# Down products in another order, constants inside the product stream, and idle products during the load, in a hybrid encoder block

## The chip, the core and the metric

The kernel runs on one core of one Trainium2 chip. Its time is the device time of one launch, in microseconds (us); smaller is better. Five engines work beside each other, each on its own queue of instructions in program order: PE (TensorE, matrix products and transposes), DVE (VectorE), ACT (ScalarE), POOL (GpSimd) and SP, whose queue here issues most of the DMA transfers between HBM and the on-chip memory. An instruction waits, by semaphore, for what it needs, and everything behind it on its engine waits with it.

## The reference

One block of a bidirectional encoder over 1024 tokens of 1024 features, all in float32:

```
x = x + 1/2 * SwiGLU_1(RMSNorm(x))          # FFN 1: gate, up: 1024 -> 2816; down: 2816 -> 1024
p = RMSNorm(x) @ W_in                       # latents, mLSTM inputs, gates, two branch gates
A = MLA(p)                                  # latent attention, 8 heads, rotary key from positions
B = mLSTM(p)                                # forward and backward chunked scans, 4 heads
x = x + (sigmoid(g_A) * (A @ Wa) + sigmoid(g_B) * (B @ Wb)) @ W_out
x = x + 1/2 * SwiGLU_2(RMSNorm(x))          # FFN 2, as FFN 1
x = RMSNorm(x)
SwiGLU(h) = (silu(h @ w_gate) * (h @ w_up)) @ w_down
```

The rotary tables are sines and cosines of positions times 16 frequencies.

## The kernel before

**Precision.** A float32 matrix product is made of three products of halves: each operand is split into a high part H (an ACT copy to the type fp32r) and a low part L (the difference, on DVE), and PE adds H·H, H·L and L·H into one PSUM bank. So every operand costs an ACT and a DVE instruction before PE can use it: for weights these are L250 and L251, for the activations L367 and L368, for the down products L594 and L595.

**Products.** The large products use Strassen and Winograd's scheme: a product of 2 by 2 blocks is made of seven products, numbered 1 to 7, and sums of blocks. Tokens 0 to 511 (tiles of 128 tokens, t = 0 to 3) are the first row of blocks, t = 4 to 7 the second.

**Stages**, in order of the trace: load, norm and transposes of x (0 to 24 us); FFN 1 gate and up (24 to 460); FFN 1 down (460 to 679); narrow projections, latents, gates (to about 840); mLSTM (to 1100); attention (to 1346); branch products and merge (to 1440); the output projection, called the merged down product (1443 to 1518); FFN 2 gate and up (1532 to 1960), FFN 2 down and the last norm (to 2182).

**Load.** `rms_x` norms a token tile: a square on ACT, a small chain over DVE and POOL, and one multiplication by scale and weight, L112 on DVE, or for t = 1, 3, 5 in two later stages L109 and L110 on POOL. `combine_x` transposes the tile on PE (L363, eight 128x128 transposes against an identity), splits it (L367, L368), and for t < 4 keeps a plain copy s = H + L (POOL, L375); for t ≥ 4 it forms Winograd's sums T1 to T4 from the transposed tile and that copy. `begin(j)` issues the first products of column block j (L260 to L262, X and weight split by L250 and L251), which need only tiles t < 4. So the four late tiles are turned between calls of `begin`, and what follows them needs T2 of the last tile.

**Gate and up.** `gate_up` runs a list of items, each a group of products on one PSUM bank, and prepares the splits of weights four items ahead. A hook may be called ahead of an item.

**Constants.** `constants()` makes the rotary tables and the like: 14 small DVE instructions behind a transfer of the positions (from L684), some ACT functions, all in a tile called raw of which there are two. It is called before `pairs()`, the main part of gate and up.

**Down.** `down` makes seven products of 4 banks (one per 128 tokens, 512 columns). For FFN each product has 11 steps of 12 matmuls; for the merged product 4 steps. In each step SP loads a pair of operands, ACT and DVE split it (L594, L595), and L602 issues 12 matmuls. The order is 1, 6, 2, 5, 7, 3, 4. When a bank is done, DVE adds it to x (L624). Product 3 completes t = 0 to 3 and product 4 completes t = 4 to 7; `done(t)` then writes x out and norms the tile, and its transposes follow (L128 for FFN 1, L363 for the merged product). The steps of product 4 carry some transposes of t < 4 in FFN 1. The order of PE's instructions is chosen by a scheduler unless instructions are pinned by `keep_in_program_order`.

PSUM banks come from two groups of four (b0, b1), splits from 6 buffers, the loads from 4 (rw) and 2 (raw).

## Time and profile before

| | us |
|---|---|
| median of 3 runs | 2179.76 (2177.51 to 2180.40) |
| profiled execution | 2183.92 |
| its span, first to last instruction | 2182.1 |
| PE busy in the span | 2107.3 |
| DVE busy | 1520.4 |
| ACT busy | 954.6 |
| POOL busy | 376.5 |
| mean granted clock of PE | 0.988 |

The profile comes from one execution; the 1.8 us that it took beside its span lie before the first and after the last instruction. The clock is a share of full speed, 1 being 2.4 GHz; PE has two levels, 1.2 and 2.4 GHz, so a stretch at 0.75 was half at either. PE is not busy in 2182.1 - 2107.3 = 74.8 us of the span; 11.6 us of that lie behind its last instruction.

### The profile page before, as it was taken

The numbers are of one execution on the slowest core, as the hardware profiler recorded it, in microseconds if no ns is written. First come the engines' busy times: TensorE is split into PE (matmuls) and PEld (weight loads), VectorE is DVE, ScalarE is ACT, GpSimd is POOL, SyncE is SP. The second block draws the span as 40 slices with busy tenths as digits, with TensorE's granted clock in tenths as the row PEclk, the third lists the DMA queues.
The fourth block names the chain that finished last, engine by engine and source line by source line (L and its number), as shares of the span: only waits on it lengthen the run. The fifth ranks groups of instructions, "written<-read, shape, count | busy, mean of one in ns | idle before, by whom it ended". The sixth has DMA issues, their size and how long they took to land.

```text
span 2182.1 us, 27814 instructions
## 1 busy us (share of the span) xinstructions
PE 2107.3 (97%) x10091; PEld 1761.1 (81%) x10091; DVE 1520.4 (70%) x2205; ACT 954.6 (44%) x1493; POOL 376.5 (17%) x319
## 2 busy tenths in 40 slices
PE   6899999999998999999999999998999999999997
PEld 5788888888886888888888888877788888888886
DVE  6788777765476566366658887667788877774565
ACT  5433333334444334544368885235533333324344
POOL 3000000000013655243445442002300000000001
PEclk9999999999998999999999999999999999999999
DMA  8567544486553333222441103975567744557545
GB/s 231 171 209 237 190 164 164 172 305 193 174 193 111 121 111 123 81 88 88 153 150 49 40 11 124 332 258 171 169 216 240 241 157 153 178 206 239 194 147 188
DMA packets 249337, 367.85 MB, mean 169 GB/s; under 512 B 24048, under 2 KB 133488, under 8 KB 249200
## 3 DMA queue, kind: packets, MB, share of 16 engines
q1 hardware_dynamic: 244016, 355.60, 49.5%
q10 hardware_dynamic: 4608, 8.39, 1.0%
q8 instruction: 79, 1.29, 0.2%
q0 software_dynamic: 576, 2.10, 0.2%
q14 instruction: 58, 0.48, 0.1%
HBM read 254.28 MB, written 111.74 MB: 168 GB/s over the span
## 4 chain that ended last, share of the span: by engine, by line
PE 42%; DVE 8%; ACT 3%; issue 2%; DMA 2%; POOL 2%; DVEq 0%; SPq 0%; ACTq 0%; POOLq 0%
PE pb L602 11%; PE pb L261 5%; PE pb L262 5%; PE pb L260 5%; PE pP L1237 2%; PE pav L1245 1%; PE pSc L83 1%; PE pav L1246 1%; DVE s L271 1%; PE pSc L84 1%; PE pSc L85 1%; PE pb L83 1%; PE pb L84 1%; PE pb L85 1%; DVE w L251 1%
## 5 line engine op out<-in xcount | busy, mean ns | idle before, releaser
L602 PE MATMUL pb<-w 128*128 128x512 f32 x2184 | 501.4, 391 | 7.9 <-DVE w L595 7.9
L602 PEld LDWEIGHTS pb<-w 128*128 128x128 f32 x2184 | 410.8, 189 | 95.7 <-DVE w L595 10.3
L595 DVE TENSOR_TENSOR w<-rw,w 128x1024 fp32r<-128x1024 f32 x182 | 222.1, 1227 | 182.3 <-ACT w L594 180.8
L594 ACT ACTIVATE w<-rw 128x1024 fp32r<-128x1024 f32 x182 | 192.7, 1062 | 281.2 <-PE pb L602 262.1
L93 POOL TENSOR_TENSOR rs<-ms,mhalf 128x1 f32<-128x1 f32 (+3 forms) x52 | 61.8, 1193 | 1019.5 <-DVE ms L98 1012.8
L250 ACT ACTIVATE w<-s 128x512 fp32r<-128x512 f32 x176 | 110.8, 629 | 243.5 <-DVE s L267 192.3
L251 DVE TENSOR_TENSOR w<-s,w 128x512 fp32r<-128x512 f32 x176 | 121.6, 691 | 61.3 <-ACT w L250 61.0
L83 PE MATMUL pin<-HH,dH 128*128 128x512 f32 x384 | 152.3, 397 | 0.2 <-DVE TL L1213 0.2
L84 PE MATMUL pin<-HL,dH 128*128 128x512 f32 x384 | 150.9, 393 | 0.0
L85 PE MATMUL pin<-HH,dL 128*128 128x512 f32 x384 | 150.5, 393 | 0.0
L260 PE MATMUL pb<-XH,w 128*128 128x512 f32 x352 | 138.9, 397 | 2.3 <-ACT XH L367 1.3
L260 PE MATMUL pb<-YH,w 128*128 128x512 f32 x352 | 137.9, 394 | 0.7 <-ACT s L412 0.7
L261 PE MATMUL pb<-XL,w 128*128 128x512 f32 x352 | 137.9, 392 | 0.0
L261 PE MATMUL pb<-YL,w 128*128 128x512 f32 x352 | 137.6, 391 | 0.0
L262 PE MATMUL pb<-XH,w 128*128 128x512 f32 x352 | 137.0, 391 | 0.0
L262 PE MATMUL pb<-YH,w 128*128 128x512 f32 x352 | 137.0, 391 | 0.0
L251 DVE TENSOR_TENSOR w<-rw,w 128x512 fp32r<-128x512 f32 x144 | 102.6, 715 | 41.3 <-ACT w L250 41.2
L271 DVE TENSOR_TENSOR s<-pb,s 128x512 f32<-128x512 f32 x152 | 103.5, 686 | 19.4 <-PE pb L262 16.9
L250 ACT ACTIVATE w<-rw 128x512 fp32r<-128x512 f32 x144 | 89.0, 622 | 36.4 <-PE pb L85 12.7
L416 ACT ACTIVATE h<-s 128x512 f32<-128x512 f32 x66 | 41.8, 633 | 120.1 <-DVE s L271 120.1
L1229 POOL TENSOR_SCALAR pe<-pe,ri 128x1024 f32<-128x1024 f32 x64 | 72.0, 1126 | 112.1 <-DVE ri L1228 106.5
L1239 DVE TENSOR_TENSOR PL<-pP,PH 128x512 fp32r<-128x512 f32 x128 | 82.9, 679 | 7.2 <-ACT PH L1238 7.2
(326 smaller groups left out, 4624.9 us busy)
## 6 DMA issues: line engine op xcount, KB each, us to landing
rw<-in_ffn_w_gate SPq DMA_DIRECT2D x54, 512.0 KB, 5.9
rw<-in_ffn_w_up SPq DMA_DIRECT2D x54, 512.0 KB, 5.1
rw<-in_ffn_w_down SPq DMA_DIRECT2D x44, 512.0 KB, 3.8
rw<-f1h SPq DMA_DIRECT2D x77, 256.0 KB, 2.8
rw<-f2h SPq DMA_DIRECT2D x77, 256.0 KB, 2.7
rw<-in_ffn_w_down SPq DMA_DIRECT2D x66, 256.0 KB, 3.0
f1h<-h SPq DMA_DIRECT2D x55, 256.0 KB, 2.4
f2h<-h SPq DMA_DIRECT2D x55, 256.0 KB, 2.3
```

Of the source, the lines that this page charges most:

```text
L83: nc.tensor.matmul(ps, wH, mH, start=start, stop=False)
L84: nc.tensor.matmul(ps, wH, mL, start=False, stop=False)
L85: nc.tensor.matmul(ps, wL, mH, start=False, stop=stop)
L250: nc.scalar.activation(out=H_, in_=src, func=AF.Copy)
L251: return (H_, L_), lambda: nc.vector.tensor_tensor(out=L_, in0=src, in1=f32(H_), op=ALU.subtract)
L260: nc.tensor.matmul(ps, w[0][:, k, :], B[0][:, k, :], start=start and k == 0, stop=False, skip_group_check=True)
L261: nc.tensor.matmul(ps, w[0][:, k, :], B[1][:, k, :], start=False, stop=False, skip_group_check=True)
L262: nc.tensor.matmul(ps, w[1][:, k, :], B[0][:, k, :], start=False, stop=stop and k == 3, skip_group_check=True)
L271: eng.tensor_tensor(out=out, in0=a, in1=b, op=op)
L594: nc.scalar.activation(out=H_, in_=r, func=AF.Copy)
L595: nc.vector.tensor_tensor(out=L_, in0=r, in1=f32(H_), op=ALU.subtract)
L602: nc.tensor.matmul(banks[t], l[:, 0, ts_], r[:, 1, :], start=start and j == 0 and i == 0, stop=stop and j == n - 1 and i == 2, skip_group_ ...
```

## The change

The order of the products in `down` becomes 1, 2, 6, 5, 3, 7, 4: product 3, which completes t = 0 to 3, is fifth instead of sixth, with products 7 and 4 behind it. Product 2 accumulates on the banks of product 1, and product 3 on those of product 5, which are first copied by ACT (as before, but now directly ahead of them). The matmuls of L602 are pinned in program order, the last two steps of products 3 and 4 go bank by bank (`tails=2`). The transposes of t < 4 move into steps of product 7 (FFN 1) or of 7 and 4 (merged product). The multiplications of t = 1, 3, 5 go from POOL to DVE; the copies s in `combine_x` go from POOL to ACT. `constants()` is hooked ahead of the items of j = 6 and has a tile of its own. In FFN 2, `begin(0)` comes ahead of the late tiles, so no `begin` stands behind the last of them. During the load, 29 products of the identity with itself are issued between the transposes (14, 3, 3, 3, 6). Three blocks of narrow columns (`small_cols`) instead of two are issued ahead of the gates.

```diff
 in rms_x callers:   rms_x(t, w, xn_tile(t), t in (1, 3, 5))  ->  rms_x(t, w, xn_tile(t))
...
@@ combine_x
-            p_ = R.bank(1).rearrange("p (k t) -> p k t", k=4)
+            p_ = R.bank(group).rearrange("p (k t) -> p k t", k=4)
...
-            for n, s in zip(("B11", "B21"), kept[i]):
-                nc.gpsimd.tensor_tensor(out=s, in0=f32(X[n][0][:, :, c]), in1=f32(X[n][1][:, :, c]), op=ALU.add)
+            for v, s in zip(ps, kept[i]):
+                nc.scalar.activation(out=s, in_=v, func=AF.Copy)
@@ gate_up
-                    hooks[j]()
+                    in_order(hooks[j])
@@ down, products
-                    nc.tensor.matmul(banks[t], l[:, 0, ts_], r[:, 1, :], start=start and j == 0 and i == 0,
-                                     stop=stop and j == n - 1 and i == 2, skip_group_check=True)
+                    tc.keep_in_program_order(nc.tensor.matmul(
+                        banks[t], l[:, 0, ts_], r[:, 1, :], start=start and j == 0 and i == 0,
+                        stop=stop and j == n - 1 and i == 2, skip_group_check=True))
@@ down
-        u2 = [R.sum() for _ in range(4)]
-        for t in range(4):
-            nc.scalar.activation(out=u2[t], in_=a[t], func=AF.Copy)
+        u2 = copies(a)
+        run(2, a, False, True, each=lambda t: add(xo[t][:, lo], a[t], xo[t][:, lo]))
         b = [R.bank(1) for _ in range(4)]
-        run(6, b, True, True, each=lambda t: into(nc.vector, u2[t], b[t], u2[t], ALU.add))
-        run(2, a, False, True, each=lambda t: add(xo[t][:, lo], a[t], xo[t][:, lo]))
-        c = [R.bank(1) for _ in range(4)]
+
+        def c12_first(t):
+            into(nc.vector, u2[t], b[t], u2[t], ALU.add)
+            add(xo[t][:, hi], u2[t], xo[t][:, hi])
+        run(6, b, True, True, each=c12_first)
+        c = [R.bank(0) for _ in range(4)]
         run(5, c, True, True)
...
+        p5 = copies(c)
+
+        def c12(t):
+            add(xo[t][:, hi], c[t], xo[t][:, hi])
+            done(t)
+        run(3, c, False, True, each=c12, tails=2)
+        d = [R.bank(1) for _ in range(4)]
+        step7, step4 = between()
...
-        run(7, d, True, True, each=c22)
-
-        def c12(t):
-            add(xo[t][:, hi], c[t], xo[t][:, hi])
-            done(t)
-        run(3, c, False, True, each=c12, tails=last, raw=R.raw)
+        run(7, d, True, True, each=c22, step=step7, raw=R.raw)
...
-        run(4, e, True, True, each=c21, step=step, tails=last, raw=R.raw)
+        run(4, e, True, True, each=c21, step=step4, tails=2, raw=R.raw)
@@ FFN 1
-        begin, pairs = gate_up(R, X, *fw1, comb)
+        begin, pairs = gate_up(R, X, *fw1, comb, {6: constants})
...
+        def busy(n):
+            b = R.bank(0)
+            for _ in range(n):
+                tc.keep_in_program_order(nc.tensor.matmul(b[:, 0:P], ident, ident, start=True, stop=True))
+        busy(14)
...
-                    combine_x(R, t, xn.pop(t), X, kept)
+                    combine_x(R, t, xn.pop(t), X, kept, t % 2)
+                    busy(3 if t < 3 else 6)
...
-        constants()
         pairs()
...
-                if t in (5, 6):
+                if t > 4:
                     early[t - 5] = small_cols(t - 5, R.bank(1))
...
-                if 1 <= j < 5:
-                    mix_turn(j - 1)
-            return step
+                if 4 <= j < 8:
+                    mix_turn(j - 4, 0)
+            return step, None
@@ merged product and FFN 2
-            for t in range(4):
-                combine_x(R, t, xn.pop(t), X2, kept)
+            def step7(j):
+                if j == 2:
+                    turn(0, 0)
+
+            def step4(j):
+                if j < 2:
+                    turn(2 * j + 1, 1)
+                if j == 0:
+                    turn(2, 1)
+            return step7, step4
...
+        begin(0)
         for t in range(4, NT):
-            begin(t - 4)
+            begin(t - 3)
             combine_x(R, t, xn.pop(t), X2, kept)
-        begin(4)
         pairs()
```

The rows that follow are of the instruction order of each kernel: line, operation, output <- inputs with buffer numbers, size. Lines from 124 on stand a few numbers higher in the changed kernel.

On DVE, in the load: L112 is the norm's multiplication (into raw, t = 2 and t = 3), L368 makes the low part of a turned tile, L251 that of a weight. Before:

```order
L112 SCALAR_TENSOR_TENSOR raw_316<-x_314,rs_321,nw_258 128x1024
L251 TENSOR_TENSOR w_375<-rw_370,w_375 128x512
L368 TENSOR_TENSOR XL0_240<-pb_301,XH0_239 128x4x128
L251 TENSOR_TENSOR w_394<-rw_372,w_394 128x512
L251 TENSOR_TENSOR w_412<-rw_370,w_412 128x512
L112 SCALAR_TENSOR_TENSOR raw_344<-x_342,rs_349,nw_258 128x1024
L251 TENSOR_TENSOR w_427<-rw_372,w_427 128x512
```

And in the changed kernel:

```order
L112 SCALAR_TENSOR_TENSOR raw_339<-x_337,rs_344,nw_273 128x1024
L98 TENSOR_SCALAR ms_374<-ss_372 128x1
L368 TENSOR_TENSOR XL0_240<-pb_315,XH0_239 128x4x128
L368 TENSOR_TENSOR XL0_240<-pb_320,XH0_239 128x4x128
L112 SCALAR_TENSOR_TENSOR raw_371<-x_369,rs_376,nw_273 128x1024
L251 TENSOR_TENSOR w_409<-rw_404,w_409 128x512
L251 TENSOR_TENSOR w_428<-rw_406,w_428 128x512
```

The multiplication of t = 3 has moved ahead of the first three splits of weights.

On PE, at the end of FFN 1's last product: L602 is the down product into the four banks of t = 4 to 7 (numbers pb_5311 to pb_5314 before), L128 turns the normed tile of t = 4. Before:

```order
L602 MATMUL pb_5311<-w_5564 128x512
L602 MATMUL pb_5312<-w_5564 128x512
L602 MATMUL pb_5313<-w_5564 128x512
L602 MATMUL pb_5314<-w_5564 128x512
L602 MATMUL pb_5311<-w_5565,w_5564 128x512
L602 MATMUL pb_5311<-w_5564,w_5565 128x512
L602 MATMUL pb_5312<-w_5565,w_5564 128x512
L602 MATMUL pb_5312<-w_5564,w_5565 128x512
L602 MATMUL pb_5313<-w_5565,w_5564 128x512
L602 MATMUL pb_5313<-w_5564,w_5565 128x512
L602 MATMUL pb_5314<-w_5565,w_5564 128x512
L602 MATMUL pb_5314<-w_5564,w_5565 128x512
```

And in the changed kernel (banks pb_5423 to pb_5426, of which the one of t = 5, pb_5424, is last):

```order
L128 MATMUL psT_5628<-ident_72,xn_5620 128x128 x4
L128 MATMUL psT_5635<-ident_72,xn_5620 128x128 x4
L602 MATMUL pb_5424<-w_5601 128x512
L602 MATMUL pb_5424<-w_5602,w_5601 128x512
L602 MATMUL pb_5424<-w_5601,w_5602 128x512
L602 MATMUL pb_5424<-w_5608 128x512
L602 MATMUL pb_5424<-w_5609,w_5608 128x512
L602 MATMUL pb_5424<-w_5608,w_5609 128x512
L128 MATMUL psT_5658<-ident_72,xn_5650 128x128 x4
L128 MATMUL psT_5665<-ident_72,xn_5650 128x128 x4
L128 MATMUL psT_5713<-ident_72,raw_5705 128x128 x4
L128 MATMUL psT_5720<-ident_72,raw_5705 128x128 x4
```

The banks no longer end within eight matmuls of each other: three are done early, 24 matmuls of the narrow columns and the turn of t = 4 stand between them and the fourth, and the turns of t = 5 and 6 follow the fourth at once.

On PE, from the merged product to FFN 2: L363 turns t = 0 to 3, L260 is the first product of `begin(0)`. Before:

```order
L602 MATMUL pb<-w 128x512 x336
L363 MATMUL pb<-ident,xn 128x128 x16
L363 MATMUL pb<-ident,raw 128x128 x16
L260 MATMUL pb<-YH_13477,w 128x512 x3
L363 MATMUL pb<-ident,xn 128x128 x4
```

And in the changed kernel:

```order
L602 MATMUL pb<-w 128x512 x253
L363 MATMUL pb<-ident,xn 128x128 x8
L602 MATMUL pb<-w 128x512 x41
L363 MATMUL pb<-ident,xn 128x128 x8
L363 MATMUL pb<-ident,raw 128x128 x4
L602 MATMUL pb<-w 128x512 x3
L363 MATMUL pb<-ident,raw 128x128 x4
L602 MATMUL pb<-w 128x512 x15
L363 MATMUL pb<-ident,raw 128x128 x8
L602 MATMUL pb<-w 128x512 x4
L260 MATMUL pb<-YH_13406,w 128x512
L602 MATMUL pb<-w 128x512 x20
```

The 32 transposes that stood behind the last product now stand inside products 7 and 4.

## Rows read from the trace of the kernel before

**Rows 1.** What each engine was busy for, from the page, part 1

```profile
PE 2107.3 (97%) x10091; PEld 1761.1 (81%) x10091; DVE 1520.4 (70%) x2205; ACT 954.6 (44%) x1493; POOL 376.5 (17%) x319
```

**Rows 2.** The waits of PE: engine line waited for: total us, times, longest

```profile
PE pb L363 <- DVE xn L112: 10.4, 3, 8.0
PE pb L602 <- DVE w L595: 7.9, 4, 4.5
PE pb L363 <- DVE raw L112: 6.1, 2, 3.2
```

**Rows 3.** Windows by stage: busy us (instructions) per engine, granted PE clock, DMA share

```profile
86.00:96.00 10.00, 4.54 (x11) 3.36 (x12) 7.11 (x13) 3.20 (x7) 0.00 (x0) 0.73 0.60 197
...
682.00:690.00 8.00, 6.09 (x23) 5.45 (x24) 6.68 (x8) 2.88 (x6) 5.29 (x4) 0.50 0.29 114
...
1518.00:1540.00 22.00, 13.63 (x54) 10.92 (x55) 20.85 (x28) 11.37 (x23) 20.59 (x15) 0.69 0.63 201
...
1600.00:1870.00 270.00, 269.32 (x1186) 221.96 (x1185) 219.28 (x343) 90.68 (x156) 0.00 (x0) 1.00 0.58 193
```

**Rows 4.** Timeline of PE, load stage: start, us, instruction, idle before

```profile
21.18 1.94 PE L363 MATMUL pb<-ident,raw 128*128 128x128 f32 x8 [3.21 <-DVE raw L112]
24.45 2.07 PE L260 MATMUL pb<-XH,w 128*128 128x512 f32 x4 [1.33 <-ACT XH L367]
...
27.17 0.63 PE L260 MATMUL pb<-XH,w 128*128 128x512 f32 x1
...
28.88 0.56 PE L261 MATMUL pb<-XL,w 128*128 128x512 f32 x1
```

**Rows 5.** Timeline of DVE, load stage

```profile
17.01 2.83 DVE L251 TENSOR_TENSOR w<-rw,w 128x512 fp32r<-128x512 f32 x2
19.76 1.27 DVE L112 SCALAR_TENSOR_TENSOR raw<-x,rs,nw 128x1024 f32<-128x1024 f32 x1
```

**Rows 6.** Timeline of PE, first feed-forward, transposes to T2

```profile
88.10 0.50 PE L260 MATMUL pb<-T2H,w 128*128 128x512 f32 x1 [2.42 <-ACT T2H L367]
91.96 0.80 PE L261 MATMUL pb<-T2L,w 128*128 128x512 f32 x1 [3.35 <-DVE T2L L368]
```

**Rows 7.** Timeline of DVE, same stretch

```profile
73.27 0.17 DVE L684 CAST raw<-raw 128x8 f32<-128x8 int32 x1 [2.27 <-DMA raw<-in_positions]
...
87.41 0.29 DVE L700 TENSOR_SCALAR raw<-raw 128x256 f32<-128x256 f32 x1
...
90.62 0.68 DVE L368 TENSOR_TENSOR XL<-pb,XH 128x512 fp32r<-128x512 f32 x1
91.22 0.68 DVE L368 TENSOR_TENSOR T2L<-h,T2H 128x512 fp32r<-128x512 f32 x1
```

**Rows 8.** Timeline of PE, end of the first down product

```profile
663.30 3.15 PE L602 MATMUL pb<-w 128*128 128x512 f32 x8 [2.01 <-DVE w L595]
...
682.14 1.94 PE L128 MATMUL psT<-ident,xn 128*128 128x128 f32 x8 [3.32 <-DVE ms L98]
685.85 1.97 PE L128 MATMUL psT<-ident,xn 128*128 128x128 f32 x8 [1.77 <-POOL xn L110]
...
704.16 0.55 PE L883 MATMUL pc<-ident,cn 128*128 128x128 f32 x3 [3.43 <-DVE HL L131]
```

**Rows 9.** Timeline of POOL, same stretch

```profile
700.34 2.35 POOL L159 TENSOR_TENSOR dL<-raw,dH 128x1024 fp32r<-128x1024 f32 x1 [3.34 <-ACT dH L158]
```

**Rows 10.** Timeline of PE, end of the merged down product

```profile
1521.48 3.30 PE L363 MATMUL pb<-ident,xn 128*128 128x128 f32 x16 [3.51 <-DVE ms L98]
1527.26 1.71 PE L363 MATMUL pb<-ident,raw 128*128 128x128 f32 x8 [2.48 <-DVE YL L368]
```

**Rows 11.** Groups of DVE instructions in the merged down product

```profile
L595 DVE TENSOR_TENSOR w<-rw,w 128x1024 fp32r<-128x1024 f32 x25 | 30.1, 1221 | 17.6 <-ACT w L594 17.6
```

**Rows 12.** Timeline of PE and DVE, last down product and tail

```profile
2139.71 30.76 PE L602 MATMUL pb<-w 128*128 128x512 f32 x135
...
2175.69 2.48 DVE L112 SCALAR_TENSOR_TENSOR raw<-x,rs,nw 128x1024 f32<-128x1024 f32 x2 [0.67 <-POOL rs L93]
```

35 lines of the change are left out of this document (18 added, 17 removed).

## The prediction

> **What bounds the kernel now.** I read the page's busy times first. PE works in 2107.3 of 2182.1 us and DVE in 1520.4 [rows 1], so PE is the bound nearly everywhere, and only time in which PE stands still or runs at half clock can be won. The list of PE's waits says where it stands still: 16.5 us for normed tiles before transposes at L363 under two releasers, and 7.9 us in four waits of a down product for its split [rows 2]. The windows by stage give the clock: 0.73 in 86 to 96 us, 0.50 in 682 to 690, 0.69 in 1518 to 1540, against 1.00 in the undisturbed 1600 to 1870, where PE is busy 269.32 of 270 us with 1186 instructions, 0.227 us each [rows 3]. After 24 us at the half level the starts of four neighbours lie (28.88 - 27.17) / 4 = 0.43 us apart [rows 4]. So each product at the low level costs 0.2 us extra. The losses lie at five places: the load, the wait for T2 in FFN 1, the seam behind the first down product, the seam behind the merged one, and the tail. The change touches all five. The sum is made against the profiled execution, 2183.92 us (span 2182.1 and 1.8 beside it); that is 4.2 us over the median of the runs shown, 2179.76, and I take the difference found off the median.
>
> **Load: -3.5.** The last tile's transposes start at 21.18 behind a wait of 3.21 us for DVE's norm, the first product at 24.45 [rows 4]. DVE did the norm of t = 3 only at 19.76, behind a pair of weight splits that took 2.83 us [rows 5]. Now that norm stands ahead of all splits, and the copies and norms on POOL, beside which DVE ran slowly, are gone from here. Counting DVE's new order (one norm 1.27, a half-size operation 0.60 from start to start [rows 5, 7]) the first product starts near 21.9: -2.5. About twelve products ran at the low level, 24.45 to 28.88 and beyond, a loss of 12 x 0.2 = 2.4 us. PE now works without a break from the transposes of t = 3 and six idle products on, so some five of them should be saved: -1.0. Bounds: all twelve saved and the start 3.1 earlier, -5.5; no clock, and half the start, -1.0. The 29 idle products cost 0.25 us each at most (a transpose of this size took 1.94 / 8 = 0.24 [rows 4]), 7 us in all; they are hidden by the 16.5 us in which PE waited for norms anyway. Without that cover they would cost all 7.
>
> The Trainium skill (TensorE: Matmul & The Clock Gate, Part 4: PE-mode transpose) says that transposes do not count as work for the clock as matmuls do. By it only the six idle products would lead the rise, the clock's part would be -0.7 and the sum 0.3 smaller. This trace does not bear it out: 16 transposes in a row took 3.30 us, 0.21 each instead of 0.24 [rows 4, 10], so they sped up with no product among them.
>
> **T2 in FFN 1: -3.7.** PE waited 2.42 us for T2's high and 3.35 us for its low part [rows 6], and the next twelve ran slow. DVE was the cause: 14 instructions of the constants lay in its queue from 73.27 to 87.41, about 3.9 us, behind a wait of 2.27 us for the positions [rows 7]. Without them, 13 DVE operations stand between the last transposes and T2L, 13 x 0.60 = 7.8 us, against 24 products, 24 x 0.227 = 5.4 us, that cover it: a wait of about 2.3 instead of 6.1 (the two, and 0.31 before them). Net -3.8, of which I take 0.1 off for the ACT copies. The clock's loss of 2.4 I leave as it is; at best it goes too, -6.
>
> **Constants in the stream: 0.** The same 14 instructions and the wait move into the items at j = 6. Splits there run four items ahead, 4 x 12 x 0.227 = 10.9 us; 3.9 and some 2 to 3 us of waiting fit under it. If SP issues the positions late, behind loads that wait for buffers, DVE stands and PE runs dry: +10 at most by a wait twice the cover, and all that is queued behind DVE's first cast, the splits and sums, is late.
>
> **First down product: -1.7.** Of the four L602 waits the first is unchanged (4.5 us, the merged product's start). A wait of 2.01 us and the eight slow matmuls behind it, 3.15 instead of 1.8 us [rows 8], sit in a late product with the splits of the narrow weights ahead on DVE, and so does one of the 0.7 us waits. With the transposes moved to product 7, and the additions spread over more products, I expect 1 us of idle time there and no fall of the clock: -3.0. The seam behind product 4 now has 3.32 + 1.77 + 3.43 = 8.5 us of idle time [rows 8] and some 5.7 at the low level (clock 0.50 [rows 3]). In the new order of PE the bank of t = 5 is last, and the transposes of t = 5 stand right behind it: its addition, square, scale and multiplication, about 5 us, lie open. Then t = 7 waits some 2 us for DVE, and with t = 6 and 7 turned together the next weights come late: they need the tile that t = 6 held, a transfer and POOL's split, 2.35 us [rows 9], about 4 us in all. 11 us idle and 4.5 slow against 14.2: +1.3. Bounds of the seam: -3 when the narrow products cover t = 5, +4 when each of these waits pulls the clock down.
>
> **Merged product: -5.4.** From 1518 to 1540 PE executed 54 instructions, 36 of them transposes: 36 x 0.12 (half of 0.24) + 18 x 0.227 = 8.4 us at full speed, so 13.6 of 22 us were lost. Now the transposes stand inside products 7 and 4, and DVE becomes the bound there: 8 splits of 1.22 us [rows 11], 32 half-size operations of 0.60 (16 and 4 additions, 8 low parts, 4 splits) and 4 norms of 1.2 are 33.8 us, against 96 x 0.227 + 32 x 0.12 = 25.6 us of PE. So 8.2 us are lost in place of 13.6. Bounds: -10 when most of DVE's list falls behind the first product of FFN 2, +2 when each transpose waits by itself.
>
> **T2 in FFN 2: +2.9.** There was no such wait, since a whole `begin` (48 products) stood behind the last turn. Now 24 products stand there, 5.4 us against the same 7.8 of DVE: 2.0 us idle with latency, and part of a slow stretch, 0.9. Bounds 0 and 4.4.
>
> **Last down product and tail: -2.4.** The other 0.7 us wait goes (-0.6). PE ends at 2139.71 + 30.76 = 2170.47 and the last pair of norms at 2175.69 + 2.48 = 2178.17, 7.7 us later [rows 12]. With banks that end 6 x 0.227 = 1.4 us apart, one tile follows the last matmul instead of four: one multiplication of 1.24 and half a microsecond of queueing go: -1.8 (bounds -3, +1).
>
> **Edits at nothing.** The ACT copies ahead of products 2 and 3 are done bank by bank, and each bank is needed 9 products or 2 us after the copy can start; with ACT late, up to +2 at each of six places. Pinning H·L directly behind H·H asks for the low part 0.2 us after the high one instead of 0.9; it has been ready for a step, 2.7 us.
>
> **The sum.** -3.5 - 3.7 + 0 - 1.7 - 5.4 + 2.9 - 2.4 = -13.8: the profiled basis gives 2170.1, the median 2166.0.
>
> **The rivals.**
> The seams only move: DVE's list in the merged product holds PE as long as the old seam did, and the first seam loses 3 us more. For it speaks that DVE has 33.8 us of work in 25.6; against it that less than half of that list is wanted by PE at once. -13.8 + 5.4 + 1.7 = -6.7, 2173.
>
> Short waits cost no clock: the Trainium skill (the same page, Why this matters for your kernels) warns of gaps longer than each of the waits of about 2 us counted here. As a mechanism of this kernel: the T2 wait of FFN 1 leaves the clock up (-2.4 more) and FFN 2's does too (-0.9), so -17.1, 2162.7. Against it stands the wait of 2.01 us with eight matmuls at 0.39 behind it [rows 8]; for it, that the waits of 0.7 us passed without a fall.
>
> Waits at the head of PE's queue, the slower side: the turned tiles now stand at twelve places inside products, each pinned behind a norm on DVE, and ready matmuls wait behind them. A wait of 2 us with eight slow matmuls costs 2.0 + 1.35 = 3.4 us [rows 8]. Six such waits more than counted give -13.8 + 20.4 = +6.6, 2186; it decides from the fifth or sixth on. DVE's full list in the merged product speaks for it, the slack of two whole products for t < 4 against.
>
> The constants are not hidden, so that the change moves a stall and doesn't remove it: +10, 2176, no measurable difference.
>
> **Chances.** Forecast 0.52, seams only move 0.18, short waits free 0.12, head of the queue 0.10, constants not hidden 0.08. A measurement tells 0.2%, 4.4 us, from no change: faster is under 2175.4, slower over 2184.1. With the spread of each case: faster 0.78, same 0.12, slower 0.10. The range leaves out the slower rival and the sum of all favourable bounds: 2153 to 2181.
>
> **What would show it.** First product before 22.5 us; one wait for T2 of 2 to 3 us in each FFN; no wait of PE at the constants; in the merged product PE waits inside product 7 and 4 for DVE, and FFN 2's first products run at full clock; 5 us of idle time ahead of the turn of t = 5; last norm under 6.5 us behind PE. It is wrong if the seams together keep their old loss, or if PE waits at more than three turned tiles inside a product.

## The result, and the profile after

The changed kernel takes 2169.96 us in the median (2169.08 to 2171.19) where the kernel before took 2180.4 beside it (2177.51 to 2185.62, five runs of each): a ratio of 0.995, interval 0.9935 to 0.9964. Of the 13.8 us that were forecast 10.4 came. The profiled executions differ by more, 2183.92 against 2169.08, because the one of before lies 3.5 us above its median and the one of after 0.9 below. The stages are compared between profiles, so they add up to 14.8 us; a second profile of each kernel, among the experiments, shows which of the differences come again.

The page of the kernel after, part 1, answers to [rows 1]:

```profile
PE 2106.4 (97%) x10149; PEld 1760.4 (81%) x10149; DVE 1505.6 (69%) x2211; ACT 962.5 (44%) x1509; POOL 326.8 (15%) x291
```

PE's busy time is nearly that of before, 2106.4 against 2107.3 us, but it now holds 58 records of the idle products, which fill 10.0 us. So of the 14.8 us of span that went, 3.9 are time in which PE did none of the kernel's work (74.8 us before, 60.9 + 10.0 now), and 10.9 are the same work done in less time. POOL lost 50 us, the norms and copies that went to DVE and ACT. DVE got the norms and is yet 15 us less busy. Part of the reason shows in the load: four splits take 2.49 us there now (below), where two took 2.83 in [rows 5].

The waits of PE in the kernel after (engine, line waited for, total us, times, longest) answer to [rows 2]:

```profile
PE pb L602 <- DVE sg L1344: 5.7, 1, 5.7
...
PE psT L128 <- DVE xn L112: 4.4, 1, 4.4
...
PE pb L260 <- ACT s L412: 4.2, 7, 2.8
PE pb L261 <- DVE T2L L368: 2.7, 2, 1.9
PE pb L260 <- ACT w L250: 2.4, 1, 2.4
...
PE pb L363 <- DVE raw L112: 0.6, 1, 0.6
...
PE pb L363 <- DVE xn L112: 0.5, 1, 0.5
```

The two lines of L363 that had 16.5 us are down to 1.1; idle products now fill some of that time. New are 4.4 us before L128 (the turn of t = 5), 2.8 us at L412 (the constants) and 2.4 us at L250 (T2 of FFN 2).

Landmarks of both traces, read from PE's timeline, give the time by stage. Each is the start of a stage's first matmul, unless the table says otherwise. The fifth column is the forecast's term; the last one is the difference between a second profile of each kernel:

| stretch | before | after | difference | forecast | repeated |
|---|---|---|---|---|---|
| start to the turn of t = 7 | 78.6 | 72.4 | -6.2 | -3.5 | -6.5 |
| to T3, behind T2 | 21.3 | 16.3 | -5.0 | -3.7 | -3.5 |
| to the first down product (constants) | 360.7 | 363.8 | +3.1 | 0 | +2.5 |
| first down, seam, narrow products | 414.7 | 409.6 | -5.1 | -1.7 | -4.7 |
| mLSTM, attention | 470.7 | 470.0 | -0.7 | 0 | -2.6 |
| branch products, and merged product to its first wait's end | 96.6 | 94.4 | -2.3 | 0 | -1.9 |
| merged product, FFN 2 with T2 | 517.2 | 517.4 | +0.2 | -5.4 + 2.9 | +1.7 |
| FFN 2 down, to the start of PE's last matmul | 210.2 | 212.7 | +2.5 | -0.6 | +2.5 |
| tail | 12.1 | 10.7 | -1.4 | -1.8 | -1.4 |

The load answers to [rows 4]. PE's timeline of the kernel after (start, us, instruction, idle time before it):

```profile
1.37 6.03 PE L763 MATMUL pb<-ident 128*128 128x128 f32 x28 [1.37 <-POOL ident masks.py:199]
7.88 1.09 PE L363 MATMUL pb<-ident,xn 128*128 128x128 f32 x8 [0.48 <-DVE xn L112]
...
19.72 1.19 PE L260 MATMUL pb<-XH,w 128*128 128x512 f32 x4 [1.30 <-ACT XH L367]
21.39 0.50 PE L261 MATMUL pb<-XL,w 128*128 128x512 f32 x1 [0.48 <-DVE XL L368]
```

The first product starts at 19.72 instead of 24.45, and at the full level: eight transposes take 1.09 us instead of 1.94, and one product 0.50 and then 0.39 us where it took 0.63 in [rows 4]. The level is told here by these durations: the granted clock in the profile reads 1.00 up to 30 us in both kernels, also where a product takes 0.63. DVE's timeline answers to [rows 5]; the norm of t = 3 now stands ahead of the weights:

```profile
14.65 1.27 DVE L112 SCALAR_TENSOR_TENSOR raw<-x,rs,nw 128x1024 f32<-128x1024 f32 x1
15.85 2.49 DVE L251 TENSOR_TENSOR w<-rw,w 128x512 fp32r<-128x512 f32 x4
```

In the kernel before, DVE was also slower there. Its norm of t = 2, which takes 1.27 us now:

```profile
13.61 2.28 DVE L112 SCALAR_TENSOR_TENSOR raw<-x,rs,nw 128x1024 f32<-128x1024 f32 x1
```

At T2 of FFN 1, [rows 6], the waits of 2.42 and 3.35 are now 0.38 and 1.94, and nine products behind them still run at the low level (0.63). PE's timeline after:

```profile
79.34 0.50 PE L260 MATMUL pb<-T2H,w 128*128 128x512 f32 x1 [0.38 <-ACT T2H L367]
81.78 0.61 PE L261 MATMUL pb<-T2L,w 128*128 128x512 f32 x1 [1.94 <-DVE T2L L368]
82.20 0.63 PE L262 MATMUL pb<-T2H,w 128*128 128x512 f32 x1
```

The constants [rows 7] lie at 259 us now, and there PE does stop once. DVE's timeline after, the first and the last of 14 instructions ahead of the sine, and a sum of a weight (L267) some instructions behind it:

```profile
258.96 0.17 DVE L690 CAST cst<-cst 128x8 f32<-128x8 int32 x1 [0.45 <-DMA cst<-in_positions]
...
263.17 0.29 DVE L706 TENSOR_SCALAR cst<-cst 128x256 f32<-128x256 f32 x1
...
265.44 0.68 DVE L267 TENSOR_TENSOR s<-rw 128x512 f32<-128x512 f32 x1
```

ACT's timeline after, with the sine (L707), the split of that sum (L250) and the copy of a PSUM bank that the next product needs (L412):

```profile
263.49 0.42 ACT L707 ACTIVATE cs<-cst 128x256 f32<-128x256 f32 x1 [9.03 <-DVE cst L706]
266.23 0.63 ACT L250 ACTIVATE w<-s 128x512 fp32r<-128x512 f32 x1 [2.32 <-DVE s L267]
266.77 0.58 ACT L412 ACTIVATE s<-pb 128x512 f32<-128x512 f32 x1
```

And PE's:

```profile
267.40 0.50 PE L260 MATMUL pb<-XH,w 128*128 128x512 f32 x1 [2.79 <-ACT s L412]
```

DVE waited only 0.45 us for the positions, so the feared late transfer did not happen. What did: the whole chain stood in DVE's queue ahead of the weight's sum, which ended at 266.12; on ACT the split of that sum waited 2.32 us for it, and behind that split stood the copy that PE wanted. The sine, too, stood at the head of ACT's queue, for 9.03 us, but it was done at 263.91, so by this trace it was not what ended last.

The seam behind the first down product [rows 8], PE after:

```profile
685.69 1.55 PE L128 MATMUL psT<-ident,xn 128*128 128x128 f32 x8 [4.39 <-DVE xn L112]
...
693.20 0.90 PE L896 MATMUL pc<-ident,cn 128*128 128x128 f32 x3 [1.74 <-DVE HL L131]
695.40 0.80 PE L83 MATMUL pin<-HH,dH 128*128 128x512 f32 x1 [1.30 <-ACT dH L158]
```

The wait for the turn of t = 5 is there with 4.39 us (5 forecast), 1.74 and 1.30 follow, and the wait of 2.01 us inside the product is gone. Behind the merged product [rows 10] the transposes no longer stand in a block. PE after, the waits at its end and then at T2 of FFN 2:

```profile
1503.72 0.66 PE L363 MATMUL pb<-ident,raw 128*128 128x128 f32 x4 [1.80 <-ACT s L375]
1504.92 0.72 PE L363 MATMUL pb<-ident,raw 128*128 128x128 f32 x4 [0.54 <-ACT s L375]
...
1573.42 0.62 PE L260 MATMUL pb<-T2H,w 128*128 128x512 f32 x1 [2.41 <-ACT w L250]
1574.83 0.80 PE L261 MATMUL pb<-T2L,w 128*128 128x512 f32 x1 [0.79 <-DVE T2L L368]
1576.03 0.79 PE L262 MATMUL pb<-T2H,w 128*128 128x512 f32 x1 [0.41 <-DVE w L251]
1576.62 0.63 PE L260 MATMUL pb<-T2H,w 128*128 128x512 f32 x1
```

The seam itself shrank to the 2.3 us of the first two rows, with 0.7 in two short waits of L602 ahead of them. T2 of FFN 2 waits 3.6 us in three pieces, and twelve products, up to 1580.04, run at the low level. The longest piece, 2.41 us, is for a weight's split, which stood on ACT behind T2's high part. Both came late in part because DVE stood 2.71 us for a weight's transfer (2.91 in the second profile) ahead of the operations that form T2, about 1 us of it after their own inputs were there. DVE's timeline:

```profile
1569.89 0.69 DVE L267 TENSOR_TENSOR s<-rw 128x512 f32<-128x512 f32 x1 [2.71 <-DMA rw<-in_ffn_w_gate]
```

The last down product [rows 12] has two new waits; PE's timeline after:

```profile
2097.98 35.65 PE L602 MATMUL pb<-w 128*128 128x512 f32 x156 [1.36 <-DVE ms L98]
2135.20 21.83 PE L602 MATMUL pb<-w 128*128 128x512 f32 x95 [1.57 <-DVE w L595]
```

And DVE there, at the first of the two waits, and at the end:

```profile
2094.32 2.47 DVE L112 SCALAR_TENSOR_TENSOR xn<-x,rs,nw 128x1024 f32<-128x1024 f32 x2
2096.71 1.22 DVE L595 TENSOR_TENSOR w<-rw,w 128x1024 fp32r<-128x1024 f32 x1
...
2162.18 1.28 DVE L112 SCALAR_TENSOR_TENSOR raw<-x,rs,nw 128x1024 f32<-128x1024 f32 x1 [0.73 <-POOL rs L93]
```

Two norms of finished tiles stand ahead of the split that PE waits for. The last norm ends at 2163.46, 6.4 us behind PE's last matmul (2135.20 + 21.83) instead of 7.7.

### The profile page after: what moved, and what is told of

Its sections match the earlier page's. It is cut to its first block, busy times and chain, and to the rows that moved or that the text cites. A ratio compares the mean times of both kernels' runs of the same rounds, so it can differ in the third digit from the quotient of the medians.

```text
span 2167.3 us, 27899 instructions
## 1 busy us (share of the span) xinstructions
PE 2106.4 (97%) x10149; PEld 1760.4 (81%) x10149; DVE 1505.6 (69%) x2211; ACT 962.5 (44%) x1509; POOL 326.8 (15%) x291
## 4 chain that ended last, share of the span: by engine, by line
PE 78%; DVE 11%; ACT 4%; issue 3%; DMA 2%; POOL 1%; SPq 0%; ACTq 0%; POOLq 0%; DVEq 0%
PE pb L602 21%; PE pb L262 10%; PE pb L261 10%; PE pb L260 10%; PE pin L83 3%; PE pin L84 3%; PE pin L85 3%; DVE s L271 2%; PE pP L1250 2%; DVE w L251 2%; DVE s L267 2%; PE pb L83 2%; PE pb L84 2%; PE pb L85 2%; ACT w L250 1%
## 5 line engine op out<-in xcount | busy, mean ns | idle before, releaser
L602 PE MATMUL pb<-w 128*128 128x512 f32 x2184 | 504.1, 392 | 9.5 <-DVE sg L1344 5.7
L602 PEld LDWEIGHTS pb<-w 128*128 128x128 f32 x2184 | 411.0, 189 | 97.3 <-DVE sg L1344 6.1
L595 DVE TENSOR_TENSOR w<-rw,w 128x1024 fp32r<-128x1024 f32 x182 | 222.0, 1222 | 179.3 <-ACT w L594 179.3
L594 ACT ACTIVATE w<-rw 128x1024 fp32r<-128x1024 f32 x182 | 193.0, 1061 | 282.4 <-PE pb L602 261.3
L250 ACT ACTIVATE w<-s 128x512 fp32r<-128x512 f32 x176 | 110.7, 630 | 238.0 <-DVE s L267 185.8
L251 DVE TENSOR_TENSOR w<-s,w 128x512 fp32r<-128x512 f32 x176 | 121.5, 691 | 60.4 <-ACT w L250 59.9
L260 PE MATMUL pb<-XH,w 128*128 128x512 f32 x352 | 137.2, 392 | 4.8 <-ACT s L412 3.5
L260 PE MATMUL pb<-YH,w 128*128 128x512 f32 x352 | 137.4, 392 | 0.7 <-ACT s L412 0.7
L251 DVE TENSOR_TENSOR w<-rw,w 128x512 fp32r<-128x512 f32 x144 | 97.9, 685 | 39.4 <-ACT w L250 39.3
L250 ACT ACTIVATE w<-rw 128x512 fp32r<-128x512 f32 x144 | 89.2, 627 | 36.0 <-DMA rw<-in_w_branch_b 14.8
```

The lines of the kernel that those rows point to most:

```text
L250: nc.scalar.activation(out=H_, in_=src, func=AF.Copy)
L251: return (H_, L_), lambda: nc.vector.tensor_tensor(out=L_, in0=src, in1=f32(H_), op=ALU.subtract)
L260: nc.tensor.matmul(ps, w[0][:, k, :], B[0][:, k, :], start=start and k == 0, stop=False, skip_group_check=True)
L594: nc.scalar.activation(out=H_, in_=r, func=AF.Copy)
L595: nc.vector.tensor_tensor(out=L_, in0=r, in1=f32(H_), op=ALU.subtract)
L602: tc.keep_in_program_order(nc.tensor.matmul(banks[t], l[:, 0, ts_], r[:, 1, :], start=start and j == 0 and i == 0, stop=stop and j == n - ...
```

## The experiments

Theories: A, the gain is made in the load and at T2, and the new order of the down products gives about as much as it costs; B, within the load, the order of DVE's queue does it and the idle products do little. The rival to A is the forecast's own split (two thirds of the gain from the down products), the rival to B that the clock does it. Ratios are against the kernel before, timed on the same chip in the same rounds.

**The changed kernel without the idle products.**

```diff
-        busy(14)
...
-                    busy(3 if t < 3 else 6)
```

> The changed kernel without its 29 idle products in the load, all else kept. Theory A: the idle products raised PE's clock. The first transposes took 1.97 us for eight before and 1.09 now, and the first twelve products 0.43 and 0.23 us. Without them the transposes take 1.9 us again and some twelve products cost 0.2 us more each: the first product starts 0.5 to 1 us later and FFN 1's first late turn some 3 us later; 2.5 to 3.5 us slower than the changed kernel, median near 2173. Theory B: the order of DVE alone (norm of t = 3 ahead of the splits, nothing on POOL) made the gain, the clock rises by itself with the denser stream: within 0.5 us of the changed kernel, near 2170.

Measured: 2169.63 us, ratio 0.9944 (0.993 to 0.9958), no different from the whole change; the intervals are too wide to show 1 us. PE's timeline of this kernel:

```profile
16.17 1.97 PE L363 MATMUL pb<-ident,raw 128*128 128x128 f32 x8 [0.49 <-DVE raw L112]
19.76 2.08 PE L260 MATMUL pb<-XH,w 128*128 128x512 f32 x4 [1.62 <-ACT XH L367]
21.64 0.73 PE L261 MATMUL pb<-XL,w 128*128 128x512 f32 x1
...
82.88 0.50 PE L261 MATMUL pb<-T2L,w 128*128 128x512 f32 x1 [1.95 <-DVE T2L L368]
83.22 0.40 PE L262 MATMUL pb<-T2H,w 128*128 128x512 f32 x1
```

The transposes are at the low level again, yet the first product starts at the same 19.76. Eight products run low until 23.45, and the turn of t = 7 comes 1.1 us later. That is the worth of the idle products at that point: 1.1 of the 6.2 us. In this profile it does not reach the end, because here the same T2 wait, 1.95 us, is followed by products at full clock, which gave the 1.1 us back; as the runs below show, the clock behind that wait changes from execution to execution, so this is luck of one execution. Theory B stands as far as the idle products go. Whether it is the order of DVE's queue, or that no copies run on POOL beside it, this run does not separate.

**The constants in five pieces**, at the items of j = 5 to 9 instead of all at j = 6; the transfers come with the first piece, the sine with the last.

```diff
-        begin, pairs = gate_up(R, X, *fw1, comb, {6: constants})
+        begin, pairs = gate_up(R, X, *fw1, comb, {5 + i: constants for i in range(5)})
```

> The changed kernel with the constants cut in five pieces, ahead of the items of j = 5 (the transfers), 6, 7, 8 (4 to 7 small DVE instructions each) and 9 (the sine on ACT). Theory A: the one block held ACT's queue for 9 us behind the sine's wait for DVE, and PE waited 2.8 us at 267 us for a copy behind it; in pieces no wait is left: FFN 1's down starts near 449.7 instead of 452.5, 2.8 us faster, median near 2167. Theory B: it is DVE's 4 us of work, in a stage where DVE has little to spare, that PE pays for: the wait comes back in smaller ones, no difference beyond 0.5 us, 2170.

Measured: 2168.64 us, ratio 0.9934 (0.992 to 0.9948), an interval that overlaps that of the change. In the profile the stretch from T3 to the first down product took 362.1 us instead of 363.8, with no wait longer than 1.0. 1.4 us over the 360.7 of before remain, so the truth lies between the two theories: 1.7 of the 3.1 us go. The pieces shorten what stands in one block on DVE and move the sine off the head of ACT's queue at once, so the run does not tell one from the other.

**The last `begin` of FFN 2 behind the last turn again**, as before the change.

```diff
-        begin(0)
         for t in range(4, NT):
-            begin(t - 3)
+            begin(t - 4)
             combine_x(R, t, xn.pop(t), X2, kept)
+        begin(4)
```

> The changed kernel with the order of FFN 2's first products as it was before: each begin ahead of one late turn, and the last begin behind the last of them. Theory A: the waits of 2.41, 0.79 and 0.41 us for T2 and the twelve slow products behind them (12 x 0.2) come from the missing 48 products of cover; they go, about 5 to 6 us faster, median near 2164.5. Theory B: the turn of t = 4, now 48 products earlier, waits for its norm at the end of the merged product instead, and the late turns press DVE sooner: a wait of 2 to 4 us there, 0 to 2 us faster, 2168 to 2170.

Measured: 2163.98 us, ratio 0.9912 (0.9895 to 0.9929), wholly below the interval of the change. The wait at T2 of FFN 2 is gone, with the low clock behind it. Windows of the kernel after, then of this one (window, length, busy us of PE, PEld, DVE, ACT, POOL, granted clock, share and GB/s of DMA). The kernel after:

```profile
1566.00:1582.00 16.00, 12.39 (x41) 8.99 (x41) 12.02 (x20) 6.51 (x12) 0.00 (x0) 0.79 0.91 311
```

This kernel, in the same window:

```profile
1566.00:1582.00 16.00, 15.96 (x71) 12.89 (x70) 13.27 (x23) 5.91 (x11) 0.00 (x0) 1.00 0.78 249
```

The stretch from the merged product's first wait to FFN 2 down takes 513.3 us instead of 517.4: T2 of FFN 2 costs 4.1 us, and without it the change would have gained 3.9 us there (before: 517.2).

**The load part alone**: the kernel before with the idle products, the copies on ACT and the constants at j = 6, and the old order of the down products.

```diff
-        begin, pairs = gate_up(R, X, *fw1, comb)
+        begin, pairs = gate_up(R, X, *fw1, comb, {6: constants})
...
-                    combine_x(R, t, xn.pop(t), X, kept)
+                    combine_x(R, t, xn.pop(t), X, kept, t % 2)
+                    busy(3 if t < 3 else 6)
```

> The kernel before with one part of the change alone: the load (idle products, norms and copies off POOL in the load and the late turns of FFN 2's copies, alternating banks) and the constants at j = 6. The down products, their order and the order of FFN 2 stay as before. Theory A: the parts add up, and FFN 1's down starts at 452.5 as in the changed kernel, 8.1 us earlier than before; from there on the old waits return: 8 us faster than before, ratio 0.9963, near 2172 where before is at 2180. So the new order of the down products is worth only the 2 us that remain. Theory B: the new order of the down products made most of the 10 us: this kernel is at most 4 us faster than before, 2176 or more.

Measured: 2170.52 us, ratio 0.9943 (0.993 to 0.9956). That is the ratio of the whole change, so the down products in the new order, together with the moved `begin` of FFN 2, give nothing on balance that these intervals would show. By stage, against this kernel, the change's down products took 1.4 us less in the first (409.6 against 411.0), 0.5 less in the merged stretch (517.4 against 517.9), 2.5 more in FFN 2 down (212.7 against 210.2) and 1.4 less in the tail. This shows theory A, with one limit: the run before this one, the new order without the moved `begin`, lies wholly below this kernel (0.9895 to 0.9929 against 0.993 to 0.9956). So the order alone does give something, 6.5 us in the medians and 4.2 in the profiles, and the `begin` takes it away. In the profile this kernel gains 12.7 us against the kernel before up to T3 and loses 2.7 at the constants; 3.7 more come in the first down product, though its order is the old one. There the wait of 3.43 us in [rows 8], with eight low products behind it, has become one of 1.35 us for another operand, with none:

```profile
692.77 0.51 PE L85 MATMUL pin<-HH,dL 128*128 128x512 f32 x1 [1.35 <-POOL dL L159]
```

Why PE's order differs at this place was not tried.

**The constants alone**: the kernel before with `constants` hooked at j = 6 in its own tile.

```diff
-        begin, pairs = gate_up(R, X, *fw1, comb)
+        begin, pairs = gate_up(R, X, *fw1, comb, {6: constants})
...
-        constants()
         pairs()
```

> The kernel before with one edit: the constants in a tile of their own, ahead of the items of j = 6. Theory A: the constants' transfers, 1 POOL and 14 DVE instructions were in the way of both the load and T2, so that this alone gives T2's part (6.1 us of waits become 2 to 2.5) less the wait of about 2.5 us in the stream, and a start of the first product between the old 24.45 and the new 19.7 us: 3 to 5 us faster than before. Theory B: the first product's delay is from POOL's copies and DVE's order, T2 from DVE's total work: less than 2 us faster.

Measured: 2178.51 us, ratio 0.999 (0.9981 to 0.9998). T3 comes 7.6 us earlier than in before, but the stretch to the first down product takes 365.6 us, 4.9 longer, so that product starts 2.7 us earlier. The profiled execution ends 4.6 us earlier, the median is 1.3 under the 2179.85 of before in the same rounds. The first product starts at 22.88: moving the constants brings 1.6 of the 4.7 us there (1.0 against the second profile of before, 23.92), the rest of the load part another 3.0 (it is 19.86 in the run with all of it). Of that rest the idle products bring nothing (19.76 without them), so it is the copies taken off POOL or the alternating banks of the transposes, which were not run apart.

**The changed kernel once more**, with no edit, for what differs between two executions of one program.

> The changed kernel itself, profiled again. In the first profile its wait of 1.94 us for T2 was followed by nine slow products, and the wait of 2.08 us at the start of the branch products by none; in the kernel before that same wait of 2.08 us was followed by seven. Theory A: whether PE's clock falls after a wait of about 2 us differs from execution to execution; the waits come back with the same lengths and the clock behind one of them otherwise, which is 1.6 to 1.8 us each. Theory B: the kernel settles it; the same slow products at the same places, span within 0.5 us of 2167.3.

Measured: 2168.46 us, ratio 0.9956 (0.9941 to 0.997), and a span of 2163.3 where the first profile had 2167.3. PE's timeline of the first profile, at the start of the branch products:

```profile
1332.16 0.50 PE L83 MATMUL pb<-bH,w 128*128 128x512 f32 x1 [2.08 <-ACT w L250]
...
1332.73 0.40 PE L83 MATMUL pb<-bH,w 128*128 128x512 f32 x1
```

And of the second:

```profile
1329.79 0.50 PE L83 MATMUL pb<-bH,w 128*128 128x512 f32 x1 [2.08 <-ACT w L250]
...
1330.65 0.63 PE L84 MATMUL pb<-bL,w 128*128 128x512 f32 x1
1331.07 0.63 PE L83 MATMUL pb<-bH,w 128*128 128x512 f32 x1
```

The wait is the same to the hundredth, and once no product ran low behind it, once seven did (granted clock 1.00 and 0.50). The wait at the start of the merged product (L1344) was 5.66 us in one and 2.52 in the other.

**The kernel before once more**, with no edit.

> The kernel before, profiled again. Theory A: whether PE's clock falls after a wait of about 2 us differs from execution to execution: the waits of 2.08 us (branch products), 2.01 us (down) and 0.6 to 3.4 us elsewhere come back with the same lengths, and the slow products behind at least one of them do not. Theory B: the same waits are followed by the same slow products, and the span is within 0.5 us of 2182.1.

Measured: 2180.64 us, ratio 1.001 (1.0 to 1.002), span 2177.0 where the profile shown above had 2182.1. Its waits at T2 were 2.01 and 3.36 us (2.42 and 3.35 in [rows 6]), six products ran low behind the 2.08 us wait, and the wait at the start of the merged product was 2.68 us instead of 4.49. So single stages differ by 1 to 3 us between executions of one program, and of the table's lines those of the load, the constants, the first down product, FFN 2 down and the tail agree within 0.6 us, the others are known to 1 or 2 us only.

**The sums and norms of FFN 2 down (and the sums of FFN 1 down) spread over the steps of products 7 and 4**, to take the two waits of 1.36 and 1.57 us away.

```diff
-        run(4, e, True, True, each=c21, step=step4, tails=2, raw=R.raw)
+        run(4, e, True, True, each=c21, step=spread, tails=2, raw=R.raw)
...
+            return (lambda j: finish(j - 2) if 2 <= j < 6 else None), None
```

> The changed kernel with DVE's work around the last three down products spread out: in FFN 2 the last norms of t = 0 to 3 run one in each of the steps 2 to 5 of product 7, and in both FFNs 12 of the 20 sums and additions behind product 7 run two in each step of product 4. Theory A: the waits of 1.36 and 1.57 us inside FFN 2's down come from DVE's and ACT's lump of norms and additions ahead of the next splits; spread, they go: FFN 2's down takes 210 instead of 212.7 us, 2.5 to 3 us faster, median near 2167. Theory B: they come from the loads into the pair of raw buffers that product 7 and 4 use (a new load waits for its predecessor's split); they stay, within 0.5 us of 2170.

Measured: 2167.37 us, ratio 0.9948 (0.9936 to 0.9959). Both waits are there with the same 1.36 and 1.57 us: around the waits DVE's instructions come in the old order, as the scheduler chose it. The run decides nothing on the waits.

**The same, with DVE's sums, the norms' squares and the splits L594 and L595 pinned in program order.**

```diff
-                nc.vector.tensor_tensor(out=L_, in0=r, in1=f32(H_), op=ALU.subtract)
+                pinned(nc.vector.tensor_tensor(out=L_, in0=r, in1=f32(H_), op=ALU.subtract))
```

> The changed kernel with the work behind the last products of FFN 2's down spread out as meant in the run before last, where the scheduler had put DVE's instructions back into the old order: now the splits, the squares and the 12 sums and additions are pinned where they are written (one norm per step of product 7, two additions per step of product 4). Theory A: the waits of 1.36 and 1.57 us come from the lump on DVE and ACT ahead of the next splits: they go, FFN 2's down takes 210 instead of 212.7 us, 2.5 to 3 us faster than the changed kernel. Theory B: they come from the pair of raw buffers or from the pinned products themselves: they stay, and the kernel is within 0.5 us of the changed one.

Measured: 2199.75 us, ratio 1.0097 (1.0082 to 1.0113). What I expected is wrong. PE's timeline of this kernel in FFN 2 down:

```profile
1953.82 21.37 PE L602 MATMUL pb<-w 128*128 128x512 f32 x86 [11.48 <-DVE w L595]
```

DVE's timeline, at the start of it:

```profile
1951.93 0.69 DVE L271 TENSOR_TENSOR h<-h,s 128x512 f32<-128x512 f32 x1 [6.44 <-DMA f2h<-h]
1952.54 3.49 DVE L595 TENSOR_TENSOR w<-rw,w 128x1024 fp32r<-128x1024 f32 x3
```

The pins hold the first splits behind the last sum of gate and up, which waits 6.44 us for a transfer to free its tile, so PE stands for 11.48 us. Later each group of sums stands ahead of splits that used to overtake it, and PE waits at the starts of products (3.94 us once, 1.69 at three others). The list of waits has 22.7 us under L595 in nine waits. Letting splits run ahead of sums, which the scheduler does by itself, is worth more than the two waits.

**The turn of t = 4 moved behind the next tile's bank**, so that no pin holds the bank of t = 5 behind it.

```diff
-            if t >= 4:
-                mix_turn(t, 0)
-                if t > 4:
-                    early[t - 5] = small_cols(t - 5, R.bank(1))
+            if t > 4:
+                mix_turn(t - 1, 0)
+                early[t - 5] = small_cols(t - 5, R.bank(1))
...
+        mix_turn(7, 0)
```

> The changed kernel with the turn of t = 4 to 7 behind FFN 1's last product issued one tile later (the turn of t = 4 after the products of t = 5, and so on). Theory A: the bank of t = 5 was last because its products are pinned behind the instruction traced before them, which is the turn of t = 4, and that turn waits for a norm; so the addition and norm of t = 5 began 6 us late and PE waited 4.39 us. With the pin behind a product instead, the banks end in order, the narrow products cover the norms, and the wait goes: the stretch from the start of FFN 1's down to the mLSTM's first product takes 405.5 to 406.5 instead of 409.6 us, 3 to 4 us faster. Theory B: the next thing, the weights behind the turns (transfer, ACT, POOL), is late by as much: 0 to 1 us.

Measured: 2165.64 us, ratio 0.994 (0.9928 to 0.9953). PE's timeline of this kernel at the seam:

```profile
683.39 0.66 PE L128 MATMUL psT<-ident,raw 128*128 128x128 f32 x4 [1.60 <-DVE HL L131]
...
685.91 1.97 PE L128 MATMUL psT<-ident,raw 128*128 128x128 f32 x8 [0.60 <-DVE HL L131]
...
690.63 0.80 PE L83 MATMUL pin<-HH,dH 128*128 128x512 f32 x1 [2.12 <-ACT dH L158]
```

The four waits of the seam, with another of 0.60 among them, add up to 4.9 us instead of 8.4 (the 7.4 of the three rows above and three short ones), and the stretch takes 405.7 us instead of 409.6, in both profiles of the change. The profile shows the cause; the timed interval overlaps that of the change.

**All together.** First the pieces of constants and the last `begin` behind the last turn in both feed-forwards (with the spread that did nothing); of FFN 1:

```diff
-            begin(t - 3)
+            if t > 4:
+                begin(t - 4)
             combine_x(R, t, xn.pop(t), X, kept)
+        begin(4)
```

> All the mends together: the changed kernel with the constants in five pieces, with the last begin behind the last late turn in both FFNs, and with the spread work of the run before this one. Theory A: each takes its own wait away: -1.5 (constants), -4 (FFN 1's T2: 0.4 + 1.9 of waiting and nine slow products), -5 (FFN 2's T2), -2.7 (down): 13 us under the changed kernel, median near 2157. Theory B: where the waits for T2 go, the next thing late is DVE itself, full in both stretches, and the four late turns wait for their norms: half of it, 2162 to 2164.

Measured: 2155.54 us, ratio 0.9889 (0.9876 to 0.9902), the best of all, and faster than the change by more than either interval. In both feed-forwards T2 waits no more: T3 starts at 84.53 instead of 88.72, and the stretch behind the merged product's first wait takes 512.8 us. What FFN 1's share is worth at the end the profile does not show: a wait of 1.84 us with eight low products comes at the constants, the first down product starts at 448.95, 0.3 us ahead of the run with the pieces alone (449.22), and the mLSTM starts 2.2 us later than in that run. Then the same with the late turn and the pinned spread:

> All mends in one kernel: constants in pieces, the last begin behind the last late turn in both FFNs, the pinned spread in FFN 2's down, and the late turn in FFN 1. The version with the first two (and the spread that did not take effect) had a median of 2155.5. Theory A: the two new mends add 2.7 and 3.5: median near 2149.5. Theory B: one of them is hidden behind another wait: 2152 to 2155.

Measured: 2183.07 us, ratio 1.0014 (1.0005 to 1.0023): the pins cost what they cost above (22.0 us of waits under L595). The first seam was again 405.5 us. The version with the late turn and without the pins was not run.

## Why the prediction was right, and where not

The sign and the range were right, and the time lies 4 us above the forecast. The bill within it was not: the load and T2 brought 11.2 us against 7.2 forecast (9.9 in the repetition), everything else 3.6 (3.8) against 6.6. By the table the stages that did better than forecast did so by some 10 us together, those that did worse by some 9; that these nearly cancel is luck.

- *Load, -3.5.* The step was right in kind and too small: -6.2. It lies beyond the bound of -5.5 that the step gave itself. The step counted a norm of 1.27 us and half-size operations of 0.60 as the gain of DVE's new order (the 2.5 needs two of these) and named DVE's slow running beside POOL without a price. The trace has one: while POOL's copies ran, the norm of t = 2 took 2.28 us and the two splits of [rows 5] 2.83, where the same instructions take 1.27 and 1.28 without, 2.6 us together. The first product came 4.7 us earlier, not 2.5; by the two partial kernels 1.6 of it come with the constants' move and 3.1 with the rest of the load part, of which the idle products have nothing (19.76 without them). The clock's part was near, 1.1 us by the run without idle products against 1.0 forecast, though not as counted: the step took five of twelve low products as saved, and all of the eleven went (24.45 to 28.88), but short waits took part of it back. The idle products filled 10.0 us, not the 7 at most, hidden as forecast. Of transposes alone the runs show both: the 16 in a row of [rows 10] sped up at the end (their starts lie 0.21 us apart, the last three's 0.11, so that the 0.24 and 0.21 of the prediction understate it), while without the idle products four groups of eight with waits of 0.5 to 1.2 us between them stayed at 1.97. The second agrees with the rule of the Trainium skill (TensorE: Matmul & The Clock Gate, Part 4: PE-mode transpose) that transposes don't count as work for the clock, the first does not.
- *T2 of FFN 1, -3.7.* Idle time of 2.3 us was forecast and 0.38 + 1.94 measured: this step was right. The stretch gained 5.0, since nine instead of twelve products ran low; in the second profiles it gained 3.5, with the clock otherwise.
- *Constants, 0.* This step failed: +3.1 (+2.5 repeated). The step counted DVE's 3.9 us and SP's transfer, both under the cover of four items, and left out ACT's queue. What stands behind the chain on DVE has that lead, but on ACT its split waits at the head of the queue (2.32 us), and behind it stand the copies of PSUM banks, which have no lead of four items; PE waited 2.79 us for one. That the DVE block, and not the sine, ended last is read from the trace; no run separates them.
- *First down product, -1.7.* Measured -5.1. The waits came as forecast (4.39 for the turn of t = 5, the 2.01 gone). But with the old order, too, the stretch took only 411.0 us in the run with the load part alone, so the new order has 1.4 us of it, near the -1.7. The rest is the wait of 3.43 us and its low products, which went with the load part; why was not tried.
- *Merged product -5.4 and T2 of FFN 2 +2.9.* Together +0.2 (+1.7 repeated) instead of -2.5. T2 cost 4.1, within its bound of 4.4, but not by the forecast's count of DVE's operations alone: the longest wait, 2.41 us, was for a weight's split, and DVE stood for a transfer ahead of it. The seam gained 3.9 instead of 5.4, and the step's mechanism did not show: DVE's list of 33.8 us was to hold PE for 8.2, and PE waited 3.1 us in four waits there (8.4 before), 2.3 of them for ACT's copies s.
- *Last down product, -0.6.* This step failed: +2.5. It took the one wait of 0.7 us as gone and did not look for what comes ahead of the splits on DVE when product 3 is fifth: its norms and the sums of product 7 now fall into products whose splits have no other cover. This is read from DVE's rows; neither attempt to take the waits away did so. Tail: -1.4 against -1.8.
- *Edits at nothing.* The ACT copies ahead of products 2 and 3 showed no wait of PE (the copies s did, 2.3 us at the merged seam). The pins had a price that was only half seen: the order's rows showed the bank of t = 5 last, but not that the cause was a pin behind the turn of t = 4, worth 3.9 us by the run with the late turn.
- *The rivals.* Seams only move: true of FFN 2's T2 and down, not of the merged seam. Short waits cost no clock: undecided as a rule. The Trainium skill (the same page, Why this matters for your kernels) warns only of longer gaps than these; here waits of 1.94 to 2.08 us were followed by a low clock in some executions and not in others. Constants not hidden: true in kind, at 3 us, not 10. The head of PE's queue: two waits at turned tiles inside the merged product, 1.80 and 0.54 us, where the rival wanted six of 2.

Left open: the copies off POOL, the order of DVE's queue and the alternating banks were not run apart, though most of the gain comes with them. The medians differ by 10.4 us where the profiles differ by 14.8 and 13.7. The clock behind the 2 us waits and the wait at the start of the merged product vary from execution to execution and are of this size, but no run shows them over many executions.

## What to carry to other kernels

When work is moved under cover, list it on every engine that it touches: an in-order queue is held by its first waiting instruction, and here a split that waited 2.32 us on ACT held a copy that PE needed at once. Keep a whole block of independent products behind the last instruction that builds an operand; half a block cost 4.1 us in FFN 2, and the best version has it back in both feed-forwards. Pin as little as possible: a pin ties an instruction to whatever was written before it, and here pinned splits lost the run-ahead that had hidden their loads.

## What the runs showed of the hardware that was not expected

The same wait, to 0.01 us, is followed by different clocks: 2.08 us by none or by seven low products in two profiles of one program, 1.94 or 1.95 us at T2 of FFN 1 by none (without idle products, constants in pieces, load part alone) or by six to nine (the change twice, and four of its variants). Seven to nine low products cost 1.4 to 1.8 us at 0.2 each. The idle products, 29 of them in 58 records, brought the transposes of a tile from 1.97 us to 1.09 and left the time where it was, within the intervals.
